# Turning the gated GLA output and half of the mixed activation by transposing DMAs of 16-bit words, in a two-layer encoder kernel

## The chip, the cores and the metric

The kernel runs on one core of a Trainium2 chip. The time is the device time of one execution in microseconds; of a kernel that ran several times the median is given. TensorE (PE) multiplies matrices, VectorE (DVE), ScalarE (ACT) and GpSimd (POOL) work on rows of up to 128 partitions, and SyncE (SP) issues the DMAs. Instructions of one engine run in the order in which they stand; engines wait for each other by semaphores.

## The reference

A trunk of two layers over 256 tokens of width 1024, all in float32. Per layer, cut to what matters here:

```
u = rms_norm(h) ; gq, gk, gv, gg, ra, aq, ak, av, gate_a, gate_b = split(u @ w_in)
o_gla   = rms_norm(gla(gq, gk, gv, ra)) * g_gla_out      # gated linear attention, both directions
branch_a = (o_gla * silu(gg)) @ w_o_gla
q, k    = rope(rms_norm(aq) * g_q_norm), rope(rms_norm(ak) * g_k_norm)
branch_b = attention(q, k, av) @ w_o_attn
mixed   = sigmoid(gate_a) * branch_a + sigmoid(gate_b) * branch_b
h = h + rms_norm(mixed @ w_out)
h = h + rms_norm(swiglu(rms_norm(h)))
h = h + rms_norm(sigmoid(h @ w_ple_gate) * (p[l] @ w_ple_proj))
```

## The kernel before

**Numbers in two parts.** A float32 value is held as a high part, rounded by a cast to a shorter TensorE format, and a low part, the rest. A product is three matmuls: high by high, high by low, low by high (`mm3`, whose matmuls are all recorded at L94). `split` makes the two parts: a cast on ScalarE (L110) and a subtract on VectorE (L106). This is done for the weights as they arrive and for every activation that goes into a product.

**Weights.** They come in units of 512 x 512 values (1 MB), on SP's queue, into two buffers named `raw`; `split` writes them into `wh` and `wl` (four buffers each). `Stream` keeps the order: a buffer that is released starts the next load, and the next split is cast when a `wh` is free. A unit serves 24 matmuls: four blocks of 128 rows, three products each, for two halves of 128 tokens.

**Stages.** Per layer: projections (rq, gqk, v), the attention branches running beside them as side work, then `gg` (the GLA's output gate), `gate` (the two branch gates), `merge` (both branch outputs and their mix), `wout`, `ffnin`, `ffnout`, `emb`, `ple`. The names in the profile carry the stage in which they were made: `wh_0gate` is a weight part of layer 0, cast in the gate stage. The gate stage has eight units, the merge stage eight.

**Turning activations.** An activation stands with tokens on partitions; as the left factor of the next product it needs its features on partitions. `transpose_in` turns 128 x 512 values: four TensorE transposes against an identity (L402) into a PSUM tile, then `put`, which splits the PSUM tile into the `Split` object's big tiles. A `Split` holds `makers`, the tasks that fill it, and `need` finishes them before the product that reads it. `gT` is the gated GLA output turned, `mixT` the mixed activation turned; for each there are two halves of tokens (`hf`) and two of features (`j`). `gT` is read by the first two units of the merge stage, `mixT` by `wout`.

**Order.** Side work is written as generators (`Task`): a `tick` after each six matmuls counts down, and a task goes on when its count is over; `yield 9` means nine ticks. A scheduler then sets each engine's order from the order of writing and priorities. `out_gate` computes the gated output per half `hf`: a sigmoid on ScalarE (L1156), two products on VectorE, then `turn_in`, a task of two `transpose_in`.

**Small tiles.** `t512()` gives a 128 x 512 tile from a ring of five. `rope_tables(l)` (L652) loads cosines, sines and two gains, and GpSimd multiplies them into two tables of 128 x 512 with buffers of their own. Layer 0's are made at the start, layer 1's after layer 0's merge stage. `inv_sqrt` and the tail of `row_rstd` (L452, L456) use GpSimd for the norms' roots: `rstd_0ffnout` is the scale of the norm behind layer 0's FFN.

Of the kernel before, what the change touches and what calls it, by code (L numbers as in the profile page):

```python
# [10 lines left out]
F32 = mybir.dt.float32  # L11
F32R = mybir.dt.float32r
BF16 = mybir.dt.bfloat16
AF = mybir.ActivationFunctionType
ALU = mybir.AluOpType
AX = mybir.AxisListType

P = 128
T = 256
D = 1024  # L20
DEPTH = 2
# [6 lines left out]
W = dict(r=5, z=6, s0=4, s=3, s1=9, o0=1, o=1, k=4, q=3, a0=1, a1=4, a2=4, a3=1, g=6)  # L28
# [10 lines left out]
OUT = (0, 1, 2, 3, 4, 5, 10, 6, 7, 8, 9)  # L39

WAIT_PAIR, WAIT_LAST = 9, (3, 4)
UNIT = 2112
RQ = ((0, 288), (288, 672), (672, 1056))
C_GQ, C_GK, C_GV, C_GG, C_RA = 0, 512, 1024, 2048, 3072
# [4 lines left out]
def trunk_kernel(ctx: ExitStack, tc: tile.TileContext, a: dict, out: bass.AP):  # L49
# [7 lines left out]
    nc = tc.nc  # L57
# [7 lines left out]
    smp = ctx.enter_context(tc.tile_pool(name="smp", bufs=4))  # L65
# [3 lines left out]
    part = ["start"]  # L69

    def nm(s):
        uid[0] += 1
        return f"{s}_{part[0]}_{uid[0]}"
# [10 lines left out]
    def aux():  # L84
        return accp.tile([P, 512], F32, tag="acc", name=nm("aux"))

    def t512():
        return smp.tile([P, 512], F32, tag="t512", name=nm("t512"), bufs=5)

    def small(n, tag, bufs=None):  # L90
        return smp.tile([P, n], F32, tag=tag, name=nm(tag), **({"bufs": bufs} if bufs else {}))
# [80 lines left out]
    for l in range(DEPTH):  # L172
        w = a["w_in"][l]
# [7 lines left out]
        w = a["w_ffn_in"][l]  # L181
# [179 lines left out]
    class Split:  # L361
# [26 lines left out]
        def put(self, src, k, n, t0, tn):  # L388

            split(*self.at(k, n, t0, tn), src.rearrange("p (k t) -> p k t", t=tn))  # L390

        def tok(self, k, hf):
            return [t[:, 0, :] for t in self.at(k, 1, hf * P, P)]

# [3 lines left out]
    def transpose_in(sp, src, k, n, hf, plain=None):  # L398

        ps = aux()  # L400
        for i in range(n):
            nc.tensor.transpose(ps[:, i * P : (i + 1) * P], src[:, i * P : (i + 1) * P], ident)  # L402
        with tc.high_priority(AHEAD):
            sp.put(ps[:, : n * P], k, n, hf * P, P)
        if plain is not None:
            nc.scalar.copy(plain, ps[:, : n * P])
# [15 lines left out]
    def row_rstd(parts, behind=None):  # L422
# [5 lines left out]
        for j, src in enumerate(parts):  # L428
# [9 lines left out]
            else:  # L438
                with tc.issue_after(behind.ins) if j and behind is not None else nullcontext():
                    last_square[0] = nc.scalar.activation(  # L440
                        junk[:, :n], src, AF.Square, scale=1.0 / 32.0, accum_out=ss[:, j : j + 1]
                    )
# [19 lines left out]
    def halves(t):  # L462
        return [t[:, j * 512 : (j + 1) * 512] for j in range(2)]

    def turn_in(sp, x, hf, wait, plain=None):


        def turn():
            yield wait
            for j, y in enumerate(halves(x)):  # L470
                transpose_in(sp, y, 4 * j, 4, hf, plain and plain[j])

        sp.makers[hf].append(Task(turn(), part[0]))
# [178 lines left out]
    def rope_tables(l):  # L652

        ropes = []
        tab = mid()
        cosT, sinT = (tab[:, i * 256 : (i + 1) * 256].rearrange("p (s d) -> p s d", d=P) for i in range(2))
        nc.sync.dma_start(cosT, a["rope_cos"].rearrange("(s p) d -> p s d", p=P))
        nc.sync.dma_start(sinT, a["rope_sin"].rearrange("(s p) d -> p s d", p=P))
        for i, gname in enumerate(("g_q_norm", "g_k_norm")):
            gn = gain(a[gname][l], tab[:, 512 + i * P : 512 + (i + 1) * P], P)  # L660
            rt = small(512, f"rope{i}", 1)
            ct, sn = (t.rearrange("p (s d) -> p s d", d=P) for t in (rt[:, 0:256], rt[:, 256:512]))
            nc.gpsimd.tensor_tensor(out=ct, in0=cosT, in1=gn.unsqueeze(1).broadcast_to([P, 2, P]), op=ALU.mult)
            quad = lambda t: t.rearrange("p (x y i) -> p x y i", x=2, y=2)
            for y in range(2):
                for hf in range(2):
                    nc.gpsimd.tensor_tensor(
                        out=quad(sn[:, hf, :])[:, :, y, :],
                        in0=quad(sinT[:, hf, :])[:, :, y, :],
                        in1=quad(gn)[:, :, 1 - y, :],  # L670
                        op=ALU.mult,
                    )
            ropes.append((ct, sn))
        return ropes

    def up_weights(l):

        up = mid()[0:81, :].rearrange("p (d c) -> p d c", d=2)
        wup = mid(F32R)[0:81, :].rearrange("p (d c) -> p d c", d=2)
        nc.gpsimd.memset(up, 0.0)  # L680
        for r in (0, 32, 64):
            nc.sync.dma_start(up[r : r + 16], a["w_alpha_up"][l].rearrange("d r c -> r d c"))
            nc.sync.dma_start(up[r + 16 : r + 17], a["b_alpha"][l].unsqueeze(0))
        nc.scalar.copy(wup, up)
        vsub(wup[64:81], up[64:81], wup[64:81].bitcast(F32))
        return wup
# [25 lines left out]
    def square(hf, j):  # L712
        on("act", nc.scalar.activation, t512(), hv(hf, j), AF.Square, scale=1.0 / 32.0, accum_out=ss[hf][:, j : j + 1])

# [58 lines left out]
    Task(start(), part[0])  # L773
    keep = cp.tile([P, 512], BF16, tag="keep", name="keep")
    nc.gpsimd.memset(keep, 1.0)
# [4 lines left out]
    for l in range(DEPTH):  # L780
# [3 lines left out]
        if l == 0:  # L784
            with after_start:
                ropes = rope_tables(0)
# [213 lines left out]
        for x in range(2):  # L1000
            o = project_t(uT)
            for i in range(2):
                dst = qk[:, x, 2 * i : 2 * i + 2, :]
                src = o[i].rearrange("p (h t) -> p h t", t=T)
# [143 lines left out]
        gT = Split()  # L1148

        def out_gate():  # L1150
            while not (gla.over and attention.over):
                yield 1
            for hf in range(2):
                sg = mid()
                with tc.issue_after(last_exp[0].ins):
                    nc.scalar.activation(sg, gg[:, hf, :], AF.Sigmoid)  # L1156
                for j, t in enumerate(halves(sg)):
                    s = slice(j * 512, (j + 1) * 512)
                    vmul(t, t, gg[:, hf, s])
                    vmul(t, t, on[:, hf, s])  # L1160
                turn_in(gT, sg, hf, W["g"])

        ogate = Task(out_gate(), f"{l}gg")

# [3 lines left out]
        for br in range(2):  # L1168
            t = big().rearrange("p (s c) -> p s c", s=2)
# [8 lines left out]
        mixT = Split()  # L1178
        ogate.need()
        for j in range(2):  # L1180
            for br, src in enumerate((gT, aT)):
                for hf, o in enumerate(project(src)):
                    sl = [s[:, hf, j * 512 : (j + 1) * 512] for s in sgate]
                    vmul(sl[br], o, sl[br])
                    if br == 1:
                        nc.vector.tensor_tensor(out=sl[0], in0=sl[0], in1=sl[1], op=ALU.add)

                        def turn(src=sl[0], j=j, hf=hf):
                            yield WAIT_MIX
                            transpose_in(mixT, src, 4 * j, 4, hf)  # L1190

                        mixT.makers[hf].append(Task(turn(), part[0], j))

        if l + 1 < DEPTH:
            ropes = rope_tables(l + 1)


        part[0] = f"{l}wout"
        gpost = gain(a["g_mix_post"][l], mid(), D)
# [24 lines left out]
        for hf in range(2):  # L1224
            ws.lend = hf == 1
            for b in range(2):
# [5 lines left out]
                sg = t512()  # L1232
# [75 lines left out]
        for x in FFN:  # L1308
# [7 lines left out]
            if x == "o":  # L1316
                n, w = outs.pop(0), ws.take()
# [8 lines left out]

        if l + 1 < DEPTH:
            wup_next = up_weights(l + 1)


        part[0] = f"{l}ffnout"
# [17 lines left out]
        for hf in range(2):  # L1349
            s = slice(hf * P, (hf + 1) * P)  # L1350
# [85 lines left out]
```

## Time and profile before

| what | value |
|---|---|
| median of 3 runs | 939.79 us (938.04 to 939.82) |
| the profiled execution | span 937.3 us; the page gives no further time of it |
| TensorE busy | 922.6 us, 98% of the span, 4697 instructions |
| VectorE, ScalarE, GpSimd busy | 732.4, 561.6 and 80.8 us |
| DMA, all of it | 169.26 MB, 181 GB/s over the span |
| TensorE clock granted | 0.9 or more in every slice of the span |

The profile is of one execution. Its span runs from the first to the last recorded instruction; the median is 2.5 us above it. A matmul's row has the engine, the line, the output and the two inputs, the weights' and the moving operand's shapes. Transposes on TensorE stand as matmuls with `ident`. "The chain" is the work that ended last, followed back from the end.

### The profile page before, as it was taken

Reading aid. Unit: us, or ns where it says so; the run is one execution under the profiler, and the core shown is the slowest. Engines: PE = TensorE matmul, PEld = TensorE weight load, DVE = VectorE, ACT = ScalarE, POOL = GpSimd, SP = SyncE. Lnnn points to the kernel's source line nnn. Section 1 sums busy time; section 2 is a strip of 40 time slices with the busy share of each in tenths; the row PEclk is TensorE's granted clock in tenths of the full one; section 3 lists DMA queues with packets and bytes.
Section 4 is the critical chain, followed back from the end, with each engine's and each line's share of the span. In section 5 each row is a group of like instructions: output and inputs, shape, how many; then the busy total and the mean of one; then the engine's idle time right before and its main releaser. Section 6 shows DMA issues by size and latency. Waiting matters only on the chain.

```text
span 937.3 us, 12331 instructions
## 1 busy us (share of the span) xinstructions
PE 922.6 (98%) x4697; PEld 783.9 (84%) x4697; DVE 732.4 (78%) x933; ACT 561.6 (60%) x928; POOL 80.8 (9%) x150
## 2 busy tenths in 40 slices
PE   8999999999999999999999999999999999999996
PEld 6998888888878878888899988888888788888786
DVE  4798978456569899999689799674666798989874
ACT  4669676443457565567666686754435666656563
POOL 3400214000000000000022001200001000000000
PEclk9999999999999999999999999999999999999999
DMA  6464455665275565547455525365553937463551
GB/s 229 168 223 137 136 191 191 191 213 180 91 249 169 203 233 190 203 143 249 167 175 181 192 78 180 116 244 181 200 190 103 310 114 268 154 266 112 180 180 45
DMA packets 88089, 169.26 MB, mean 181 GB/s; under 512 B 3351, under 2 KB 26391, under 8 KB 88030
## 3 DMA queue, kind: packets, MB, share of 16 engines
q1 hardware_dynamic: 88030, 168.47, 52.8%
q8 instruction: 37, 0.61, 0.3%
q14 instruction: 22, 0.18, 0.1%
HBM read 167.41 MB, written 1.05 MB: 180 GB/s over the span
## 4 chain that ended last, share of the span: by engine, by line
PE 79%; DVE 9%; DMA 4%; ACT 3%; issue 3%; POOL 1%; SPq 0%; POOLq 0%; ACTq 0%; DVEq 0%
PE acc_1ffnin L94 9%; PE acc_0ffnin L94 8%; PE acc_0gate L94 5%; PE acc_1gate L94 5%; PE acc_1merge L94 5%; PE acc_0merge L94 5%; PE acc_0ffnin L543 4%; PE acc_1ffnin L543 4%; PE acc_1gqk L94 2%; PE acc_0rq L94 2%; PE acc_0gqk L94 2%; PE acc_1ple L94 2%; PE acc_0gg L94 2%; PE acc_1gg L94 2%; PE acc_1v L94 2%
## 5 line engine op out<-in xcount | busy, mean ns | idle before, releaser
L94 PE MATMUL acc_1ffnin<-wh_1ffnin,big_1ffnin 128*128 128x512 f32 x176 | 56.9, 393 | 0.0
L94 PE MATMUL acc_0ffnin<-wh_0ffnin,big_0ffnin 128*128 128x512 f32 x176 | 56.8, 392 | 0.0
L110 ACT CAST wh_1ffnin<-raw_1ffnin 128x1024 fp32r<-128x1024 f32 x38 | 38.1, 1050 | 23.1 <-PE acc_1ffnin L94 7.7
L110 ACT CAST wh_0ffnin<-raw_0ffnin 128x1024 fp32r<-128x1024 f32 x38 | 37.9, 1049 | 22.0 <-PE acc_0ffnin L94 7.9
L106 DVE TENSOR_TENSOR wl_1ffnin<-raw_1ffnin,wh_1ffnin 128x1024 fp32r<-128x1024 f32 x38 | 44.8, 1219 | 5.6 <-ACT wh_1ffnin L110 5.4
L106 DVE TENSOR_TENSOR wl_0ffnin<-raw_0ffnin,wh_0ffnin 128x1024 fp32r<-128x1024 f32 x38 | 44.7, 1219 | 3.9 <-ACT wh_0ffnin L110 3.9
L94 PEld LDWEIGHTS acc_1ffnin<-wh_1ffnin,big_1ffnin 128*128 128x128 f32 x176 | 33.0, 188 | 7.1 <-ACT big_1ffnin L110 0.4
L94 PEld LDWEIGHTS acc_0ffnin<-wh_0ffnin,big_0ffnin 128*128 128x128 f32 x176 | 33.0, 188 | 6.7
L106 DVE TENSOR_TENSOR wl_0ffnin<-lent_0ffnin,wh_0ffnin 128x1024 fp32r<-128x1024 f32 x30 | 35.5, 1218 | 1.9 <-ACT wh_0ffnin L110 1.7
L106 DVE TENSOR_TENSOR wl_1ffnin<-lent_1ffnin,wh_1ffnin 128x1024 fp32r<-128x1024 f32 x30 | 35.4, 1218 | 2.0 <-ACT wh_1ffnin L110 2.0
L110 ACT CAST wh_1ffnin<-lent_1ffnin 128x1024 fp32r<-128x1024 f32 x30 | 30.2, 1049 | 9.0 <-PE acc_1ffnin L94 3.0
L110 ACT CAST wh_0ffnin<-lent_0ffnin 128x1024 fp32r<-128x1024 f32 x30 | 30.2, 1049 | 8.4 <-PE acc_0ffnin L94 3.7
L94 PE MATMUL acc_0ffnin<-wl_0ffnin,big_0ffnin 128*128 128x512 f32 x88 | 34.3, 389 | 0.0
L94 PE MATMUL acc_1ffnin<-wl_1ffnin,big_1ffnin 128*128 128x512 f32 x88 | 34.3, 389 | 0.0
L94 PE MATMUL acc_1ffnin<-wh_1ffnin,big_1wout 128*128 128x512 f32 x96 | 31.2, 394 | 0.0
L94 PE MATMUL acc_0ffnin<-wh_0ffnin,big_0wout 128*128 128x512 f32 x96 | 31.2, 394 | 0.0
L543 PE MATMUL acc_0ffnin<-wh_0ffnin,mid_0ffnin 128*128 128x512 f32 x96 | 31.0, 390 | 0.0
L543 PE MATMUL acc_1ffnin<-wh_1ffnin,mid_1ffnin 128*128 128x512 f32 x96 | 31.0, 390 | 0.0
L106 DVE TENSOR_TENSOR wl_0gate<-raw_0gate,wh_0gate 128x1024 fp32r<-128x1024 f32 x14 | 16.5, 1221 | 17.8 <-ACT wh_0gate L110 17.8
L106 DVE TENSOR_TENSOR wl_1gate<-raw_1gate,wh_1gate 128x1024 fp32r<-128x1024 f32 x14 | 16.5, 1221 | 17.8 <-ACT wh_1gate L110 17.8
L94 PE MATMUL acc_0rq<-wh_start,big_start 128*128 128x384 f32 (+1 forms) x96 | 25.4, 349 | 1.4 <-ACT big_start L120 1.4
L94 PE MATMUL acc_0gate<-wh_0gate,big_start 128*128 128x512 f32 x80 | 24.8, 389 | 0.0
(647 smaller groups left out, 2931.3 us busy)
## 6 DMA issues: line engine op xcount, KB each, us to landing
raw_0ffnin<-in_w_ffn_out_dram SPq DMA_DIRECT2D x11, 1024.0 KB, 5.3
raw_1ffnin<-in_w_ffn_out_dram SPq DMA_DIRECT2D x11, 1024.0 KB, 5.9
lent_0ffnin<-in_w_ffn_in_dram SPq DMA_DIRECT2D x6, 1024.0 KB, 8.7
lent_1ffnin<-in_w_ffn_in_dram SPq DMA_DIRECT2D x6, 1024.0 KB, 7.8
raw_0rq<-in_w_in_dram SPq DMA_DIRECT2D x4, 1024.0 KB, 5.2
raw_0v<-in_w_in_dram SPq DMA_DIRECT2D x4, 1024.0 KB, 5.0
raw_0gg<-in_w_in_dram SPq DMA_DIRECT2D x4, 1024.0 KB, 5.1
raw_0gate<-in_w_o_gla_dram SPq DMA_DIRECT2D x4, 1024.0 KB, 5.2
```

The source lines that it names most:

```text
L94: return nc.tensor.matmul(o, lhsT, rhs, start=start, stop=stop)
L106: nc.vector.tensor_tensor(out=out, in0=in0, in1=in1, op=ALU.subtract)
L110: nc.scalar.copy(hi, src)
L543: nc.tensor.matmul(o, x, y, start=first and k + n == 0, stop=k == 3 and n == 2, skip_group_check=not first)
```

## The change

Three edits.

- `turn_words` takes the place of TensorE's transposes for all four pieces of `gT` and for the first feature half of `mixT` (two pieces): six pieces per layer, twelve in all. A piece of 128 x 512 float32 is seen as 128 x 1024 words of 16 bits. A ScalarE copy sets the low words first and the high words behind them (`w`), a transposing DMA on SP's queue turns the eight blocks of 128 x 128 words (`r`), and a ScalarE copy interleaves the words again (`z`), which `put` splits. Between these steps it waits 3 and 9 ticks (`SENT`, `LANDED`), and between two pieces of the gated output 2 (`NEXT`). The second feature half of `mixT` stays on TensorE.
- The ring of `t512` has seven tiles instead of five; the rope tables are taken from it instead of from buffers of their own.
- Layer 1's `rope_tables` are made at the end of `ffnin`, not at the end of `merge`.

```
 WAIT_PAIR, WAIT_LAST = 9, (3, 4)
+SENT, LANDED, NEXT = 3, 9, 2
...
-        return smp.tile([P, 512], F32, tag="t512", name=nm("t512"), bufs=5)
+        return smp.tile([P, 512], F32, tag="t512", name=nm("t512"), bufs=7)
...
+        def turn_words(self, src, k, n, hf):
+            x = lambda: t512()[:, : n * P]
+            w = x()
+            w16 = w.bitcast(U16)
+            nc.scalar.copy(
+                w16.rearrange("p (s c) -> p s c", s=2), src.bitcast(U16).rearrange("p (c s) -> p s c", s=2)
+            )
+            yield SENT
+            r = x()
+            r16 = r.bitcast(U16)
+            nc.sync.dma_start_transpose(out=r16.rearrange("p (r t) -> p r t", t=P), in_=w16)
+            yield LANDED
+            z = x()
+            z16 = z.bitcast(U16)
+            nc.scalar.copy(z16.rearrange("p (c s) -> p s c", s=2), r16.rearrange("p (s c) -> p s c", s=2))
+            self.put(z, k, n, hf * P, P)
...
-            rt = small(512, f"rope{i}", 1)
+            rt = t512()
...
-                turn_in(gT, sg, hf, W["g"])
+                for j, y in enumerate(halves(sg)):
+                    gT.makers[hf].append(Task(gT.turn_words(y, 4 * j, 4, hf), part[0], j))
+                    yield NEXT
...
-                        def turn(src=sl[0], j=j, hf=hf):
+                        def turn(src=sl[0], hf=hf):
                             yield WAIT_MIX
-                            transpose_in(mixT, src, 4 * j, 4, hf)
-
-                        mixT.makers[hf].append(Task(turn(), part[0], j))
-
-        if l + 1 < DEPTH:
-            ropes = rope_tables(l + 1)
-
+                            transpose_in(mixT, src, 4, 4, hf)
+
+                        turn = turn() if j else mixT.turn_words(sl[0], 0, 4, hf)
+                        mixT.makers[hf].append(Task(turn, part[0], j))
...
             wup_next = up_weights(l + 1)
+            ropes = rope_tables(l + 1)
```

How this moves instructions is seen at two places. SP's queue, from the load of the gate stage's fourth unit (`raw_0gg_1470`) to that of its eighth (`raw_0gate_1726`), before:

```order
L257 DMA raw_0gg_1470<-in_w_in_dram 128x4x512
L657 DMA mid_0merge_2228<-in_rope_cos_dram 128x2x128
L658 DMA mid_0merge_2228<-in_rope_sin_dram 128x2x128
L257 DMA raw_0gg_1598<-in_w_in_dram 128x4x512
L328 DMA mid_0merge_2228<-in_g_q_norm_dram 128x128
L328 DMA mid_0merge_2228<-in_g_k_norm_dram 128x128
L328 DMA mid_0wout_2245<-in_g_mix_post_dram 128x1024
L328 DMA mid_0wout_2247<-in_g_ffn_pre_dram 128x1024
L257 DMA raw_0gate_1656<-in_w_in_dram 128x4x512
L257 DMA raw_0gate_1664<-in_w_in_dram 128x4x512
L328 DMA ggla_1gla_4863<-in_g_gla_out_dram 128x256
L257 DMA raw_0gate_1726<-in_w_in_dram 128x4x512
```

The rope loads and gains stand between the weights; all are plain loads. The same stretch in the changed kernel, up to the first unit of the merge stage (names are numbered anew; `t_` is a `t512` tile, and lines are two further down):

```order
L259 DMA raw_0gg_1470<-in_w_in_dram 128x4x512
L410 DMA_TRANSPOSE t_0gg_1670<-t_0gg_1632 128x8x128
L259 DMA raw_0gg_1598<-in_w_in_dram 128x4x512
L330 DMA mid_0wout_2234<-in_g_mix_post_dram 128x1024
L259 DMA raw_0gate_1654<-in_w_in_dram 128x4x512
L410 DMA_TRANSPOSE t_0gg_1692<-t_0gg_1646 128x8x128
L259 DMA raw_0gate_1662<-in_w_in_dram 128x4x512
L410 DMA_TRANSPOSE t_0gg_1720<-t_0gg_1684 128x8x128
L410 DMA_TRANSPOSE t_0gg_1734<-t_0gg_1700 128x8x128
L259 DMA raw_0gate_1708<-in_w_in_dram 128x4x512
L330 DMA mid_0wout_2236<-in_g_ffn_pre_dram 128x1024
L259 DMA raw_0gate_1748<-in_w_o_gla_dram 128x4x512
```

The rope loads are gone from here, and four transposing DMAs stand between the weights: one ahead of unit five, one between units six and seven, two ahead of unit eight (`raw_0gate_1708`).

GpSimd's queue at the end of layer 0's FFN, before:

```order
L680 MEMSET mid_0ffnin_3709 81x1024
L452 TENSOR_SCALAR rstd_0ffnout_3775<-ss_0ffnout_3774 128x1
L456 TENSOR_TENSOR rstd_0ffnout_3775<-rstd_0ffnout_3775,neghalf 128x1
L452 TENSOR_SCALAR rstd_0ffnout_3863<-ss_0ffnout_3862 128x1
L456 TENSOR_TENSOR rstd_0ffnout_3863<-rstd_0ffnout_3863,neghalf 128x1
```

And in the changed kernel (`t_0ffnin` are the rope tables, `mid_0ffnin_3709` what was loaded for them):

```order
L688 TENSOR_TENSOR t_0ffnin_3713<-mid_0ffnin_3709 128x256
L692 TENSOR_TENSOR t_0ffnin_3713<-mid_0ffnin_3709 128x2x32 x4
L688 TENSOR_TENSOR t_0ffnin_3720<-mid_0ffnin_3709 128x256
L692 TENSOR_TENSOR t_0ffnin_3720<-mid_0ffnin_3709 128x2x32 x4
L477 TENSOR_SCALAR rstd_0ffnout_3781<-ss_0ffnout_3780 128x1
L481 TENSOR_TENSOR rstd_0ffnout_3781<-rstd_0ffnout_3781,neghalf 128x1
```

The tables' ten operations now stand ahead of the norm's.

More of the change, by code (lines that the diff above doesn't have):

```diff
@@ L13 @@
 BF16 = mybir.dt.bfloat16
+U16 = mybir.dt.uint16
 AF = mybir.ActivationFunctionType
```

## The prediction

> **What bounds the kernel now.** First the page's line of busy times and the chain's shares by engine; then the stretches in which the transposes lie (the gate and merge stages of both layers), by engine; then the chain inside them.
>
> ```profile
> PE 922.6 (98%) x4697; PEld 783.9 (84%) x4697; DVE 732.4 (78%) x933; ACT 561.6 (60%) x928; POOL 80.8 (9%) x150
> PE 79%; DVE 9%; DMA 4%; ACT 3%; issue 3%; POOL 1%; SPq 0%; POOLq 0%; ACTq 0%; DVEq 0%
> ...
> 144.00:192.00 48.00, 48.00 (x226) 39.97 (x226) 29.68 (x34) 26.40 (x37) 10.38 (x15) 1.00 0.62 204
> 192.00:236.50 44.50, 44.50 (x203) 36.91 (x201) 26.63 (x28) 17.61 (x19) 0.00 (x0) 1.00 0.57 191
> 603.00:651.00 48.00, 48.00 (x225) 39.94 (x224) 29.68 (x34) 26.16 (x36) 2.77 (x5) 1.00 0.55 189
> 651.00:695.40 44.40, 44.40 (x202) 36.86 (x201) 26.63 (x28) 17.61 (x19) 0.00 (x0) 1.00 0.57 191
> ...
> 157.83 1.75 PE aux_0gg L402 x16
> 218.09 0.87 PE aux_0merge L402 x8
> 616.60 1.75 PE aux_1gg L402 x16
> 676.86 0.87 PE aux_1merge L402 x8
> ```
>
> The window rows give stretch, length, then busy time of PE, PEld, DVE, ACT and POOL, granted clock, DMA share and GB/s. TensorE is busy in the whole of all four windows at a granted clock of 1.00; VectorE has some 18 us to spare in each, ScalarE 22 to 27. So here every TensorE instruction lengthens the kernel, and a weight that comes late would do so too. The chain names the groups removed: 16 and 8 transposes per layer (layer 0's 16 last 1.75 us, 109 ns each).
>
> **Removed: 48 transposes.** 2 × (1.75 + 0.87) = 5.24 us, all on the path. Their own rows, with the pipeline's fill, read 1.91 and 1.03 us; two layers at those would be 5.88. I take the chain's 5.24.
>
> ```profile
> 157.67 1.91 PE L402 MATMUL aux_0gg<-ident,mid_0gg 128*128 128x128 f32 x16
> 159.33 0.47 PE L94 MATMUL acc_0gate<-wh_0gg,big_start 128*128 128x512 f32 x1
> 192.08 0.39 PE L94 MATMUL acc_0merge<-wh_0gate,big_0gg 128*128 128x512 f32 x1
> 217.93 1.03 PE L402 MATMUL aux_0merge<-ident,big_0gate 128*128 128x128 f32 x8
> ```
>
> **Added: two ScalarE copies a turn.** Twelve per layer, of 1024 16-bit elements a partition. None is in the trace; the nearest row is ScalarE on 1024 elements, SBUF to SBUF.
>
> ```profile
> 147.12 1.06 ACT L1156 ACTIVATE mid_0gg<-big_0gg 128x1024 f32<-128x1024 f32 x1
> 153.72 2.00 ACT L110 CAST wh_0gate<-raw_0gg 128x1024 fp32r<-128x1024 f32 x2 [3.18 <-DMA raw_0gg<-in_w_in_dram]
> 170.52 2.01 ACT L110 CAST wh_0gate<-raw_0gate 128x1024 fp32r<-128x1024 f32 x2 [2.12 <-PE acc_0gate L94]
> 154.72 3.49 DVE L106 TENSOR_TENSOR wl_0gate<-raw_0gg,wh_0gate 128x1024 fp32r<-128x1024 f32 x3
> 214.04 2.00 ACT L110 CAST wh_0merge<-raw_0merge 128x1024 fp32r<-128x1024 f32 x2 [3.43 <-PE acc_0merge L94]
> ```
>
> At 1.06 us each ScalarE goes from 26.4 to 34.9 of the gate's 48 us and from 17.6 to 21.8 of the merge's 44.5. What it delays are weight casts, and these run ahead: between 159.33 and 192.08 lie six units of 24 matmuls, 5.44 us each; the cast at 170.52 is the eighth gate unit's and waits for TensorE to release a buffer; its unit is used at 192.08 − 5.44 = 186.6. That lead of some 14 us is the cover; without it each copy would cost its 1.06. The cast and subtract behind each turn stay, reading SBUF instead of PSUM: nothing.
>
> **Added: the transposing DMA's place in SP's queue.** A turn has time: gT, whose transposes ran at 157.67, is read at 192.08; the mixed activation's first half, turned at 217.93, some 18 us later. The question is what it holds up: weights wait behind it on the same queue.
>
> ```profile
> 142.57 0.68 DVE L103 TENSOR_TENSOR mid_0gg<-mid_0gg,big_0gla 128x512 f32<-128x512 f32 x1
> 148.62 0.37 SPq L257 DMA_DIRECT2D raw_0gg<-in_w_in_dram  x1
> 155.96 2.65 SPq L257 DMA_DIRECT2D raw_0gate<-in_w_in_dram  x2
> 164.42 0.37 SPq L257 DMA_DIRECT2D raw_0gate<-in_w_in_dram  x1
> ...
> raw_0gate<-in_w_in_dram SPq DMA_DIRECT2D x2, 1024.0 KB, 4.9
> ...
> DMA packets 361, 0.17 MB, mean 169 GB/s; under 512 B 31, under 2 KB 361, under 8 KB 361
> q1 hardware_dynamic: 361, 0.17, 57.4%
> DMA packets 200, 0.41 MB, mean 410 GB/s; under 512 B 0, under 2 KB 0, under 8 KB 200
> q1 hardware_dynamic: 200, 0.41, 105.8%
> ```
>
> A packet window's rows give packets, MB and share of the 16 engines' time: the first window is one microsecond of small loads (140 to 141), the second one of weights (138 to 139).
>
> The first transposing DMA stands ahead of the load at 148.62; its words follow the product that ends at 143.25, so it is issued near 145. The second stands between the two loads of 155.96 (units six and seven), the third and fourth ahead of unit eight's, at 164.42.
>
> How long one of 256 KB holds the queue (call it t) no row shows. Below: at 410 GB/s, 0.64 us. Above: if it goes in pieces of 32 bytes, 8192 of them; the first window, of 1 us, gives 0.574 × 16 / 361 = 25.4 ns a packet of about 512 bytes, and over 16 engines at that 13.0 us. Between: 1024 rows of 256 bytes at 25.4 ns are 1.63 us, my value, since that is the size of a block's row here.
>
> Unit six lands at 155.96 + 4.9 = 160.9. Behind it come t, unit seven (1 MB at 410 GB/s, 2.6 us), 2t, unit eight (2.6) and its split (3.3: two casts and the last subtract): ready at 169.4 + 3t. It is needed at 186.6 − 1.75 = 184.9. So t up to 5.2 us costs nothing; above, 3(t − 5.2) per layer. In the merge two transposes stand between a load and the second output unit's; words ready near 214.5 and 217.5, that load's landing near 217: ready 217 + 2t + 5.9 (2.6 and 3.3 again), needed near 238.3 (192.08 + eight units of 5.44 + 0.87 is 236.5, where the output begins; its second unit follows half a unit, 2.7, later; all 0.87 sooner now). Up to 7.7 us nothing, then 2(t − 7.7). At 1.63 both are free, by 10.6 and 12 us.
>
> The row of 109 ns a block on TensorE comes first; the Trainium skill ("VectorE: DVE Perf Modes", The three transpose paths) lists a DMA transpose of a 128×128 block of 16-bit words at 1309 ns and advises TensorE wherever the result may go to PSUM. Eight blocks in turn would be an estimate of 10.5 us, and by it the sum would be 2 × (15.9 + 5.6) − 4.9 = 38 us slower, about 978. No run so far shows that price. The Trainium skill ("DMA: Bandwidth & Descriptors", Latency and other measured facts) also gives 261 GB/s to a transposing DMA, an estimate of 1.0 us, which leaves the sum as it is.
>
> **Moved: the next layer's rope tables, now at the end of the FFN's first part.** Their loads stand behind the embedding projection's and ahead of a gain; their ten POOL operations stand ahead of the one that gives the FFN's post-norm.
>
> ```profile
> 154.35 4.43 POOL L663 TENSOR_TENSOR rope_0merge<-mid_0merge 128x256 f32<-128x256 f32 x1 [5.21 <-DMA mid_0merge<-in_g_q_norm_dram]
> 158.75 1.16 POOL L667 TENSOR_TENSOR rope_0merge<-mid_0merge 128x64 f32<-128x64 f32 x4
> 159.87 0.74 POOL L663 TENSOR_TENSOR rope_0merge<-mid_0merge 128x256 f32<-128x256 f32 x1
> 160.56 1.18 POOL L667 TENSOR_TENSOR rope_0merge<-mid_0merge 128x64 f32<-128x64 f32 x4
> ...
> 425.64 0.37 SPq L257 DMA_DIRECT2D raw_0ffnin<-in_w_ple_proj_dram  x1
> 426.10 0.42 SPq L328 DMA_DIRECT2D mid_0ffnout<-in_g_ple_post_dram  x1
> mid_0ffnout<-in_g_ple_post_dram SPq DMA_DIRECT2D x1, 512.0 KB, 5.8
> ...
> 434.35 0.30 POOL L452 TENSOR_SCALAR rstd_0ffnout<-ss_0ffnout 128x1 f32<-128x1 f32 x1 [48.19 <-ACT t_0ffnout L440]
> 434.74 0.57 POOL L456 TENSOR_TENSOR rstd_0ffnout<-rstd_0ffnout,neghalf 128x1 f32<-128x1 f32 x1
> 435.51 1.41 DVE L500 SCALAR_TENSOR_TENSOR h<-mid_0ffnout,rstd_0ffnout,h 128x512 f32<-128x512 f32 x2
> 439.82 1.03 PE L402 MATMUL aux_0ffnout<-ident,h 128*128 128x128 f32 x8
> 447.52 0.39 PE L94 MATMUL acc_0ple<-wh_0ffnout,big_0ffnout 128*128 128x512 f32 x1
> ```
>
> The tables' inputs land about where that gain did, 426.1 + 5.8 = 431.9, or half a microsecond earlier. Beside three VectorE subtracts the chain took 7.4 us (154.35 to 161.74); with all operations as fast as the later ones it is 2 × (0.74 + 1.17) = 3.8. VectorE is busy there too: I take a middle end, 437.5 to 438.2. Then 0.95 for the norm (0.30 + 0.57 and a gap) and 0.7 a half of h: first half at 439.2 to 439.9, against 439.82. A stall of 0 to 0.3; taken 0.3. With the slow chain (end 439.3) it is about 1.2, with inputs 1.8 us late 3. Behind h on VectorE wait two units' splits (four subtracts of 1.17 us, as in the row of three) and those of the turned h (two of half that size, 0.6 each): 5.9 us from about 440.6 to 446.5, in time for the embedding's first product at 447.52, by 1 us. On SP the tables' loads delay the gain at 426.10 by their own small size alone, and the tables aren't read before the next layer. There is one such place, since only layer 0 makes tables for a next layer. The old place in the merge ran beside busy TensorE: nothing comes back.
>
> Seven 512-column tiles instead of five, plus the two tables' own: more turns in flight at no time of an engine.
>
> **Sum.** 937.3 (the span) − 5.24 + 0.3 = 932.4. The median shown, 939.79, is 2.5 above that span; so 934.9 us.
>
> **The rivals.**
> 1. The transposing DMA goes in small pieces, holds the queue, and weights come late. For it: pieces as small as 32 bytes give 13 us. Against: the row-sized pieces give 1.63, and the lead of units is long. Gain and loss balance at t = 5.2 + 4.94/6 = 6.0 us; above it the kernel is slower, 939.8 at 6.0 and 939.79 − 4.94 + 2 × (23.4 + 10.6) = 1002.9 at 13. Chance 0.14.
> 2. The eight blocks of one transposition are turned one after the other, each with a latency of its own. The load of 1 MB shows a fixed part of 4.9 − 2.6 = 2.3 us; were each block to pay half of it, t would be 9.2 us and the time 934.9 + 2 × (3 × 4.0 + 2 × 1.5) = 965. Against: it is one instruction on the queue, and loads of many rows pay that part once. Chance 0.08. The Trainium skill's 1309 ns a block (as above) is of this size, and its advice would be right here.
> 3. The tables on POOL hold up h: the gain is less by 1 to 3 us, 935.8 to 937.6. For it: the 4.43 us operation beside VectorE's subtracts. Chance 0.10.
> 4. TensorE's freed time isn't given back, as VectorE or ScalarE sets the pace, or t lies between 5.7 and 6.3: within 0.2%, 939.8. Against: both have 18 us or more idle in each window. Chance 0.08.
>
> **How the numbers follow.** My forecast has 0.60. About 0.2%, 1.88 us, is what a measurement of this kernel can tell from no change: 937.91 to 941.67. Rival 3 and the forecast lie below it: faster 0.70, same 0.08 (rival 4), slower 0.22 (rivals 1 and 2). The forecast's own range is 933.5 (5.88 saved with no stall gives 933.9) to 936. The whole range, for 8 in 10, leaves out 0.16 of rivals 1 and 2 above 944 (t over 6.7 us) and a little below 932.8.
>
> **What would show it.** No L402 rows under the gated output; TensorE at 100% of both stages, which end 1.75 and 0.87 us sooner per layer; casts there still released by TensorE, not by a DMA; two copies of about 1.06 us a turn; transposes landing within 5 us of issue. Wrong if casts of the gate stage wait on loads, TensorE shows gaps before a unit, or the transpose of h starts over 1 us late against the matmuls around it.

## The result, and the profile after

| | median | runs |
|---|---|---|
| changed kernel | 931.49 us | 930.93 to 933.16, 4 runs |
| kernel before, beside it | 938.91 us | 937.94 to 939.82, 4 runs |
| ratio | 0.993 | 95% interval 0.9914 to 0.9946 |

Faster by 7.4 us, where 4.9 were forecast; the time lies 1.3 us below the stated range. The two kernels were compared twice more, later: 933.51 against 938.21 us (ratio 0.9947, 0.9932 to 0.9963) and 934.49 against 938.13 us (0.9959, 0.9942 to 0.9976). So the gain is 3.6 to 7.4 us by the medians; all 16 runs of the changed kernel have a median of 933.73 us, the 61 of the kernel before in the later comparisons one of 937.90. Three of the first four runs of the changed kernel lie below all twelve later ones (932.55 and more); what set them apart isn't shown.

The page of the changed kernel, its line of busy times and the chain's shares by engine:

```profile
PE 916.4 (99%) x4649; PEld 777.9 (84%) x4649; DVE 732.8 (79%) x933; ACT 587.4 (63%) x952; POOL 82.3 (9%) x150
...
PE 81%; DVE 9%; DMA 3%; ACT 2%; issue 2%; POOL 1%; SPq 0%; POOLq 0%; ACTq 0%; DVEq 0%
```

TensorE has 48 instructions less (4697 to 4649) and 6.2 us less to do; ScalarE 24 more and 25.8 us more; VectorE stands as it was. The span is 929.6 us, the profiled execution's time 931.35, 1.75 more.

The gate and merge stages of the changed kernel, as windows from the first matmul of each stage to that of the next (columns as in the prediction's windows):

```profile
143.20:188.95 45.75, 45.75 (x207) 37.80 (x206) 29.57 (x34) 33.94 (x45) 2.74 (x4) 1.00 0.80 234
188.95:232.45 43.50, 43.50 (x193) 36.03 (x192) 26.57 (x28) 22.03 (x23) 0.00 (x0) 1.00 0.65 207
599.10:644.85 45.75, 45.75 (x206) 37.81 (x205) 29.67 (x34) 34.05 (x45) 2.73 (x4) 1.00 0.80 231
644.85:688.35 43.50, 43.50 (x193) 36.05 (x192) 26.62 (x28) 22.18 (x23) 0.00 (x0) 1.00 0.65 207
```

TensorE is still busy in the whole of every window at a clock of 1.00: nothing that was added reached it. ScalarE's 33.9 and 22.0 us are near the 34.9 and 21.8 forecast.

The limits of these windows, from the timelines of the kernel before (the first two rows) and of the changed kernel:

```profile
144.51 0.39 PE L94 MATMUL acc_0gate<-wh_0gg,big_start 128*128 128x512 f32 x1
...
236.50 0.39 PE L94 MATMUL acc_0wout<-wh_0merge,big_0merge 128*128 128x512 f32 x1
```

```profile
143.19 0.39 PE L96 MATMUL acc_0gate<-wh_0gg,big_start 128*128 128x512 f32 x1
...
188.94 0.39 PE L96 MATMUL acc_0merge<-wh_0gate,big_0gg 128*128 128x512 f32 x1
...
232.46 0.39 PE L96 MATMUL acc_0wout<-wh_0merge,big_0merge 128*128 128x512 f32 x1
```

With the row at 192.08 of the prediction, the gate stage went from 47.57 to 45.75 us and the merge from 44.42 to 43.52. The same differences between first matmuls, for seven profiles (us; "start" is the time of layer 0's first keys-and-values matmul):

| profile | start | gate 0 | merge 0 | ffnin 0 | gate 1 | merge 1 | ffnin 1 |
|---|---|---|---|---|---|---|---|
| before | 38.76 | 47.57 | 44.42 | 181.70 | 47.57 | 44.41 | 182.38 |
| before_again (same kernel) | 36.98 | 47.57 | 44.41 | 181.69 | 47.57 | 44.41 | 181.28 |
| ropes_only | 37.38 | 47.57 | 44.41 | 183.02 | 47.57 | 44.41 | 181.54 |
| gated_only | 37.99 | 45.74 | 44.43 | 182.22 | 45.74 | 44.43 | 181.49 |
| after | 37.35 | 45.75 | 43.52 | 181.37 | 45.76 | 43.52 | 181.41 |
| after_again (same kernel) | 37.82 | 45.75 | 43.52 | 182.95 | 45.75 | 43.52 | 182.48 |
| after_third (same kernel) | 37.50 | 45.76 | 43.52 | 183.96 | 45.74 | 43.52 | 181.98 |

In these profiles the gate stage is 1.82 us shorter wherever the gated output is turned by DMA, the merge 0.90 wherever the mix is, to 0.02 us: 2 × (1.82 + 0.90) = 5.44 us. What else differs is in the start and in the two FFNs, and there the same kernel differs from itself by up to 2.6 us. The whole time shows less of the gain than the stages do: 937.90 − 933.73 is 4.2 us. Where the other 1.3 us go, or whether they are scatter, is open.

The transposing DMA. Its queue's row on the page of before and then on that of after (packets, MB, share of 16 engines' span):

```profile
q1 hardware_dynamic: 88030, 168.47, 52.8%
```

```profile
q1 hardware_dynamic: 100702, 171.62, 55.8%
```

And the turn's own instructions in the changed kernel (line, count, duration in ns as least, median and greatest), with the DMAs' median time from issue to landing behind the name in the last two rows:

```profile
L410 SPq DMA_TRANSPOSE t_0gg<-t_0gg x4: 1237/1294/5613, 143.1 to 158.9; - x4
...
L410 SPq DMA_TRANSPOSE t_0merge<-t_0merge x2: 1232/1242/1252, 211.3 to 214.2; - x2
```

```profile
L404 ACT COPY t_0gg<-mid_0gg x4: 1034/1042/1058, 142.0 to 156.2; 128x1024 uint16<-128x1024 uint16 x4
```

```profile
L414 ACT COPY t_0gg<-t_0gg x4: 1348/1358/1364, 159.8 to 170.1; 128x1024 uint16<-128x1024 uint16 x4
```

```profile
t_0gg<-t_0gg SPq DMA_TRANSPOSE x4, 7.7
...
t_0merge<-t_0merge SPq DMA_TRANSPOSE x2, 3.1
```

12,672 packets more are 1056 a piece; 0.558 × 929.6 − 0.528 × 937.3 = 23.8 us of the queue's time, an estimate of 1.98 us a piece, where 1.63 was taken. A piece lands 3.1 us after its issue in the merge and 7.7 in the busier gate stage, where the prediction had looked for 5. The Trainium skill ("VectorE: DVE Perf Modes", The three transpose paths) prices a block at 1309 ns; the trace doesn't agree for eight blocks in one instruction, of which all together took 2.0 us of the queue and, in the merge, 3.1 us from issue to landing. 256 KB in 1.98 us are 132 GB/s; the trace gives half of the 261 of the Trainium skill ("DMA: Bandwidth & Descriptors", Latency and other measured facts), the lower of the two rates there.

The cover in the gate stage, from the changed kernel's timelines of SP and VectorE:

```profile
157.51 6.97 SPq L410 DMA_TRANSPOSE t_0gg<-t_0gg  x2
164.59 0.52 SPq L259 DMA_DIRECT2D raw_0gate<-in_w_in_dram  x1
```

```profile
172.37 2.36 DVE L108 TENSOR_TENSOR wl_0gate<-raw_0gate,wh_0gate 128x1024 fp32r<-128x1024 f32 x2 [2.69 <-ACT wh_0gate L112]
```

Unit eight's load goes out at 164.59, behind two transposes whose issue took SP 7 us; its split is done at 174.7 and it is used at 188.94 − 5.44 = 183.5. The lead is 8.8 us; 10.6 were forecast.

On the way, unit seven's cast waited for its load, where before it had waited for TensorE. From ScalarE's timelines, before and after:

```profile
165.08 2.01 ACT L110 CAST wh_0gate<-raw_0gate 128x1024 fp32r<-128x1024 f32 x2 [1.64 <-PE acc_0gate L94]
```

```profile
164.74 2.00 ACT L112 CAST wh_0gate<-raw_0gate 128x1024 fp32r<-128x1024 f32 x2 [2.89 <-DMA raw_0gate<-in_w_in_dram]
```

The prediction had named casts that wait on loads as a sign that it is wrong. The sign came, and TensorE didn't wait: a late cast costs only what goes beyond the lead.

The moved tables, from the changed kernel's timelines of GpSimd, VectorE and TensorE:

```profile
428.49 0.85 POOL L688 TENSOR_TENSOR t_0ffnin<-mid_0ffnin 128x256 f32<-128x256 f32 x1 [46.82 <-DMA mid_0ffnin<-in_g_q_norm_dram]
...
433.36 0.30 POOL L477 TENSOR_SCALAR rstd_0ffnout<-ss_0ffnout 128x1 f32<-128x1 f32 x1
433.75 0.57 POOL L481 TENSOR_TENSOR rstd_0ffnout<-rstd_0ffnout,neghalf 128x1 f32<-128x1 f32 x1
```

```profile
434.35 1.41 DVE L525 SCALAR_TENSOR_TENSOR h<-mid_0ffnout,rstd_0ffnout,h 128x512 f32<-128x512 f32 x2 [2.73 <-POOL rstd_0ffnout L481]
```

```profile
435.33 1.15 PE L427 MATMUL aux_0ffnout<-ident,h 128*128 128x128 f32 x8
```

The tables took 4.8 us (3.8 to 7.4 were the bounds), h came 2.7 us later than VectorE would have had it, and its first half was ready at 435.05, 0.28 us ahead of TensorE. The eight transposes took 1.15 us instead of 1.03: a stall of 0.1.

### The profile page after: what moved, and what is told of

It is laid out like the page before. It is cut to its first block, busy times and chain, and to the rows that moved or that the text cites. A ratio compares the mean times of both kernels' runs of the same rounds, so it can differ in the third digit from the quotient of the medians.

```text
span 929.6 us, 12279 instructions
## 1 busy us (share of the span) xinstructions
PE 916.4 (99%) x4649; PEld 777.9 (84%) x4649; DVE 732.8 (79%) x933; ACT 587.4 (63%) x952; POOL 82.3 (9%) x150
## 4 chain that ended last, share of the span: by engine, by line
PE 81%; DVE 9%; DMA 3%; ACT 2%; issue 2%; POOL 1%; SPq 0%; POOLq 0%; ACTq 0%; DVEq 0%
PE acc_0ffnin L96 11%; PE acc_1ffnin L96 7%; PE acc_0ffnin L568 6%; PE acc_0gate L96 5%; PE acc_1gate L96 5%; PE acc_1merge L96 5%; PE acc_0merge L96 5%; DVE wl_1ffnin L108 4%; PE acc_1ffnin L568 3%; PE acc_1gqk L96 2%; PE acc_0gqk L96 2%; PE acc_1ple L96 2%; PE acc_0rq L96 2%; PE acc_0gg L96 2%; PE acc_1gg L96 2%; PE acc_0v L96 2%
## 5 line engine op out<-in xcount | busy, mean ns | idle before, releaser
L96 PE MATMUL acc_1gate<-wh_1gate,big_0ple 128*128 128x512 f32 x80 | 24.8, 389 | 0.0
```

Source lines behind the costliest of these rows:

```text
L96: return nc.tensor.matmul(o, lhsT, rhs, start=start, stop=stop)
```

## The experiments

The question after the result: do the 2 us beyond TensorE's own 5.4 belong to the change? Theory A: no, they are scatter between executions of any of these kernels. Theory B: yes, from the ring of seven or the moved tables.

**before_again.** No edit: the kernel before.

> The kernel before, unchanged, for a second profile. Theory A (the 2 us beyond the transposes' own time are scatter between executions: the start and the last FFN's waits for weights): its start (the first six transposes near 16.1 us in the first profile, 14.9 in the changed kernel's) or its wait of 1.48 us on VectorE near 884.9 differ here from the first profile by about 1 us; the span may lie anywhere from 935.5 to 938. Theory B (those 2 us come with the ring of seven tiles or the moved tables): both stand as in the first profile within 0.3 us, span 937 to 938.

936.14 us, a single run, span 934.4, 1.1 us below what theory A allowed and 2.6 below B's. Two rows of the first profile of before, and then the same instructions in this one, from TensorE's timelines:

```profile
16.14 0.95 PE L120 MATMUL aux_start<-ident,mid_start 128*128 128x128 f32 x6
...
884.88 0.66 PE L402 MATMUL aux_1ffnin<-ident,t_1ffnin 128*128 128x128 f32 x4 [1.48 <-DVE t_1ffnin L103]
```

```profile
14.51 0.82 PE L120 MATMUL aux_start<-ident,mid_start 128*128 128x128 f32 x6
...
882.02 0.66 PE L402 MATMUL aux_1ffnin<-ident,t_1ffnin 128*128 128x128 f32 x4
```

The start is 1.6 us earlier and the wait of 1.48 us is gone, with nothing changed. In the changed kernel's profile these were the two places that had gained (14.88, no wait). So what they gave there needs no cause in the change: A, not B, for these two. What makes them differ between executions isn't shown.

**ropes_only.** The kernel before, with

```
-        ... tag="t512", name=nm("t512"), bufs=5)
+        ... tag="t512", name=nm("t512"), bufs=7)
-            rt = small(512, f"rope{i}", 1)
+            rt = t512()
         (and rope_tables(l + 1) moved from the end of merge to the end of ffnin)
```

> The kernel before with the ring of seven 512-column tiles and the rope tables taken from it and made at the end of ffnin; all transposes stay on TensorE. Theory A: as before within 1 us, 938 to 939.5. Theory B: 2 to 2.5 us faster than before, 936.5. If the tables on GpSimd hold up h (rival 3 of the prediction): 0.3 to 3 us slower, 939.2 to 942.

937.61 us against 938.21, ratio 0.9994 (0.9981 to 1.0008): no difference. B's 2 us faster are excluded by a little (the interval ends at 1.8 us faster), rival 3's slowing of 0.3 us isn't (it ends at 0.75 us slower).

**ropes_back.** The changed kernel, with

```
+        if l + 1 < DEPTH:
+            ropes = rope_tables(l + 1)          # at the end of merge again
...
-            ropes = rope_tables(l + 1)          # at the end of ffnin
```

> The changed kernel with layer 1's tables made after the merge again (still in the ring of seven). Theory A: as the changed kernel within 0.7 us, 931.5. Theory B, if the tables' place made the 2 us: 933.5. If the tables held up h in the changed kernel: 931.2 or less.

933.09 us, ratio 0.9942 (0.9928 to 0.9955), within the changed kernel's own runs. By the numbers written down beforehand this is B's 933.5; but they started from the first measurement's 931.5, and the same kernel without the edit later took 933.51 and 934.49 (below). So this run doesn't separate A from B, and shows only that the tables' place is worth nothing that these runs can tell.

**gated_only.** The changed kernel, with

```
-                        turn = turn() if j else mixT.turn_words(sl[0], 0, 4, hf)
-                        mixT.makers[hf].append(Task(turn, part[0], j))
+                        mixT.makers[hf].append(Task(turn(), part[0], j))    # turns both j on TensorE
```

> The changed kernel with the mixed activation's first half turned on TensorE again; the gated output stays with the DMAs. TensorE gets 16 transposes back, 0.9 us per layer: 931.5 + 1.8 = 933.3 under A and B alike. If the two transposing DMAs in the merge had cost anything by holding up weights, less than that: 932.5.

934.27 us, ratio 0.9954 (0.9941 to 0.9966). That is 1.0 us above the number expected, which also started from 931.5. Beside the changed kernel's median over all runs it is 0.5 us slower, which scatter hides; the table shows the 0.9 us in both merges (44.43), the gate stages shortened as before, and no more.

**after_again** and **after_third.** No edit: the changed kernel.

> The changed kernel, unchanged, beside the kernel before on the same chip, for the size of the gain. If the gain is the transposes' own time (5.4 us on TensorE): 938.2 - 5.4 = 932.8. If the first measurement's 7.4 us belongs to the change: 930.8.

> The changed kernel once more, for the size of the gain with more runs: 5.0 to 5.4 us under the kernel before beside it if the transposes' time is all of it, so 932.3 to 933.2; 930.5 to 931.5 if the first measurement's 7.4 us holds.

933.51 and 934.49 us. The first measurement's 931.49 was the low end. The gains beside the kernel before are 4.70 and 3.64 us: neither is the first measurement's 7.4, and after_third stays 1.4 us short of the 5.0 that were expected at least. After_third differs from the first profile most in layer 0's FFN (183.96 against 181.37 us); there its TensorE waits, and behind that ScalarE waits for weights. From its timeline, its waits of ScalarE between 255 and 345 us (us in total, times, longest), and the same waits in before_again:

```profile
329.45 0.47 PE L568 MATMUL acc_0ffnin<-wh_0ffnin,big_0wout 128*128 128x512 f32 x1 [1.11 <-DVE mid_0ffnin L607]
```

```profile
ACT wh_0ffnin L112 <- DMA raw_0ffnin<-in_w_ffn_in_dram: 3.7, 2, 1.9
```

```profile
ACT wh_0ffnin L110 <- DMA raw_0ffnin<-in_w_ffn_in_dram: 0.7, 1, 0.7
```

Weights of the FFN land at the edge of being needed, and these two executions wait there 3.7 and 0.7 us. It isn't the only place: in ropes_only the FFN took 183.0 us with 0.8 us of such waits. Whether the changed kernel waits there more on the average stays open: three profiles of it give 181.4, 183.0 and 184.0 us, two of the kernel before 181.7 both. Twice the turning work doesn't lengthen it: the changed kernel with copies doubled gives 181.6, with transposing DMAs doubled 181.4 (both below).

**ropes_twice.** The changed kernel, with each GpSimd operation of layer 1's tables done twice:

```
-            nc.gpsimd.tensor_tensor(out=ct, ...)
+            for _ in range(1 + (l > 0)):
+                nc.gpsimd.tensor_tensor(out=ct, ...)
-            for y in range(2):
+            for y in (0, 1) * (1 + (l > 0)):
```

> The changed kernel in which GpSimd makes layer 1's tables twice over (ten more operations, 4 to 5 us by the changed kernel's rows), ahead of the norm's root. If h ends only 0.3 us ahead of TensorE's transposes of it, as the changed kernel's rows say: 3.5 to 4.5 us slower than the changed kernel, 936. If VectorE's or the loads' later waits have room for it: within 1 us of the changed kernel.

938.96 us, 5.5 slower than after_again, 1 more than the first branch allowed. TensorE's row, and two windows, the first from within the wait:

```profile
439.53 1.50 PE L427 MATMUL aux_0ffnout<-ident,h 128*128 128x128 f32 x8 [3.28 <-DVE h L525]
```

```profile
438.00:442.00 4.00, 2.46 (x11) 2.03 (x12) 3.27 (x4) 1.52 (x3) 0.61 (x2) 0.82 0.00 0
442.00:446.00 4.00, 4.00 (x15) 3.12 (x15) 4.00 (x6) 3.30 (x7) 0.86 (x2) 0.76 0.56 179
```

The wait is there, 3.28 us. Most of the other 2.2 us is the granted clock of 0.82 and 0.76: over the 2.46 and 4.00 us that TensorE was busy in these windows, an estimate of 2.46 × 0.18 + 4.00 × 0.24 = 1.4 us. So h was at the edge in the changed kernel, as its rows said: rival 3's mechanism is there, and the changed kernel was 0.28 us short of it.

**times2** and **times3.** The changed kernel, with

```
-            nc.sync.dma_start_transpose(out=r16..., in_=w16)
+            for _ in range(2):        # times3: 3
+                nc.sync.dma_start_transpose(out=r16..., in_=w16)
```

> The changed kernel with every transposing DMA issued twice with the same words into the same tile; the second of a pair waits on SP until the first has landed. By the changed kernel's packets one holds the queue 2.0 us. If only time on the queue counts, free up to 5.2 us a turn in the gate stage: 4.0 us cost nothing, as the changed kernel, 931.5 to 932.8. If SP's waits for landings (about 5 us each, four in a gate stage) count against a lead of some 15 us: 0 to 5 us per layer, up to 942, with casts of the gate stage waiting on weight loads.

> The same with three issues of each. By queue time alone 6.0 us a turn, over the free 5.2 by 0.8: 3 x 0.8 x 2 = 4.9 us slower than the changed kernel, 937. If SP's waits count: eight landings of 5 us in a gate stage, 25 us more than the lead, per layer: 950 to 985.

times2: 932.13 us, no cost. But the repeated issues don't all stand where the sum has them. SP's timeline of times2, from unit six's load to what follows unit eight's:

```profile
152.64 0.37 SPq L259 DMA_DIRECT2D raw_0gate<-in_w_in_dram  x1
153.07 6.99 SPq L411 DMA_TRANSPOSE t_0gg<-t_0gg  x2
160.15 0.53 SPq L259 DMA_DIRECT2D raw_0gate<-in_w_in_dram  x1
161.14 1.23 SPq L411 DMA_TRANSPOSE t_0gg<-t_0gg  x1
163.65 0.38 SPq L259 DMA_DIRECT2D raw_0gate<-in_w_in_dram  x1
164.07 5.92 SPq L411 DMA_TRANSPOSE t_0gg<-t_0gg  x2
```

Three transposes stand between unit six's load and unit eight's, as many as in the changed kernel. Of the four that were added in this stage one stands ahead of unit six's load and three behind unit eight's; in times3, too, only three stand between the two loads. So neither run tests the limit of 5.2 us a turn. What times2 shows is that eight transposes in a gate stage and four in a merge cost nothing. By the pages' queue rows (58.5% of 931.1 us, 59.3% of 948.3) the second pieces took 2.2 us each of the queue and the third ones 1.5, so the 1.98 is known to about half a microsecond.

times3: 947.61 us, 14 slower, but not where it was expected: its gate stages are 45.75 us, as in the changed kernel. The merge grows by 2.7 and 4.1 us and wout by 4.1 and 5.7. From its TensorE and ScalarE timelines, and a window behind the wait:

```profile
235.44 0.50 PE L96 MATMUL acc_0wout<-wh_0merge,big_0merge 128*128 128x512 f32 x1 [2.58 <-ACT big_0merge L112]
...
243.97 0.66 PE L428 MATMUL aux_0merge<-ident,big_0gate 128*128 128x128 f32 x4 [1.84 <-DVE big_0gate L1214]
```

```profile
232.40 2.51 ACT L415 COPY t_0merge<-t_0merge 128x1024 uint16<-128x1024 uint16 x2 [4.41 <-DMA t_0merge<-t_0merge]
```

```profile
235.40:239.40 4.00, 3.96 (x10) 2.86 (x11) 3.81 (x5) 4.00 (x5) 0.00 (x0) 0.62 0.19 71
```

What comes late is the turned mix itself, not a weight: ScalarE's interleaving copies wait 4.41 us for the transposes, whose six issues stand among weight loads, and `wout` waits for the cast behind them. After 2.6 us of waiting the clock is 0.62 for 4 us; that (1.5 us, an estimate of 3.96 × 0.38) and the second wait of 1.84 are most of what `wout` grows by in layer 0. Both expectations failed on the place: queue time (937) and SP's waits ahead of weights (950 to 985).

**stores8.** The changed kernel, with eight stores of the turn's source behind each transposing DMA, into the output, which is written at the end:

```
             nc.sync.dma_start_transpose(out=r16..., in_=w16)
+            for i in range(8):
+                s = slice(i // 2 % 2 * 512, (i // 2 % 2 + 1) * 512)
+                nc.sync.dma_start(out[0, i % 2 * P : (i % 2 + 1) * P, s], src)
```

> The changed kernel in which each of the twelve turns also stores its source eight times (256 KB each) into the output, which the kernel overwrites at its end: 2 MB more per turn on SP's queue, 5.2 us at 410 GB/s. By the order, 24 of a gate stage's stores and three transposes stand between units seven's load and that of the merge's first unit. By the prediction's queue sum with 2.0 us a transpose: that unit is ready at 160.9 + 0.7 + 2.0 + 2.6 + 5.2 + 2.6 + 2 x (2.0 + 5.2) + 2.6 + 3.3 = 194.3 against 190.3 needed, in the time of the profile before: TensorE waits 4 us a layer ahead of the merge, 932.7 + 8 = 941, with casts waiting on loads of w_o_gla. If the gate stage has more lead than that sum says: within 2 us of the changed kernel. If stores are slower than loads: above 945.

965.27 us, ratio 1.0294 (1.0266 to 1.0322). From its timelines of TensorE and ScalarE, and a window of it:

```profile
195.04 1.22 PE L96 MATMUL acc_0merge<-wh_0gate,big_0gg 128*128 128x512 f32 x2 [5.50 <-ACT wh_0gate L112]
```

```profile
193.94 1.99 ACT L112 CAST wh_0gate<-raw_0gate 128x1024 fp32r<-128x1024 f32 x2 [5.74 <-DMA raw_0gate<-in_w_o_gla_dram]
```

```profile
190.00:200.00 10.00, 4.92 (x13) 3.46 (x14) 4.68 (x4) 4.47 (x5) 0.00 (x0) 0.66 0.92 323
```

This is rival 1 made real, at the place that was named: the cast of the merge's first weights waits for their load, and TensorE for the cast, 5.5 us where 4 were worked out. The queue was made long by stores, not by transposes, so this shows what a late weight does, not how long a transposing DMA holds the queue. The time fell into the third branch, above 945: the sum took 410 GB/s, and between 150 and 190 us the queue moved 271 to 331 with the DMA engines busy for 0.93 or more of each 10 us. What the sum lacked besides is what follows: slow clock, and the merge (47.7 us against 43.5) and wout (27.6 against 23.9) late in turn.

**copies_twice.** The changed kernel, each ScalarE copy of a turn in a loop of two:

```
+            for _ in range(2):
                 nc.scalar.copy(w16..., src...)
...
+            for _ in range(2):
                 nc.scalar.copy(z16..., r16...)
```

> The changed kernel with both ScalarE copies of each turn done twice (24 more copies, 29 us of ScalarE's time at 1.04 and 1.35 us). If the copies lie beside TensorE's work as the prediction says: as the changed kernel, 931.5 to 933.5. If weight casts behind them were near the edge: 1 to 10 us slower, with TensorE waiting on casts in the gate stage.

933.15 us, ratio 0.9949 (0.9929 to 0.9968): as the changed kernel. ScalarE had room for twice as much; the prediction's zero for the copies holds.

**queries_too.** A try at a faster version: the second head group's queries turned by DMA as well.

```
+        def send_q(hf):                     # w, yield SENT, transposing DMA into early[hf]
...
             for hf in range(2):
                 yield W["q"]
+                if g:                       # z from early[hf], split into qh, ql
...
-                (four TensorE transposes of the second group, each hf)
```

> The changed kernel in which the second head group's queries (two pieces of 128 x 512 per layer, 16 transposes in all) are turned by transposing DMAs too, sent while the first group's attention runs. If a turn with slack gains just TensorE's time: 16 x 0.109 = 1.75 us faster than the changed kernel's pooled 932.5, 930.8. If its two tiles or copies hold up the attention, which runs beside the projections: 932.5 or slower, with TensorE waiting in the GLA or the gate stage.

935.93 us, ratio 0.9983 (0.9969 to 0.9996): slower than the changed kernel by 2.2 us. TensorE's waits in it:

```profile
91.35 0.74 PE L96 MATMUL aux_0at<-mid_0at,big_0kv 128*128 128x512 f32 x2 [0.57 <-DVE mid_0at L108]
...
98.85 0.50 PE L96 MATMUL acc_0v<-wh_0gqk,big_start 128*128 128x512 f32 x1 [0.62 <-DVE big_0at L108]
...
547.47 0.73 PE L96 MATMUL aux_1at<-mid_1at,big_1kv 128*128 128x512 f32 x2 [0.85 <-DVE mid_1at L108]
...
554.97 0.50 PE L96 MATMUL acc_1v<-wh_1gqk,big_0ple 128*128 128x512 f32 x1 [0.66 <-DVE big_1at L108]
```

None of these is in the changed kernel: 1.2 and 1.5 us a layer of waits for the attention's VectorE work. Nor did TensorE's own work get shorter: from the first gqk matmul to the first of the merge it is busy for 0.04 and 0.13 us a layer less than in the changed kernel, not for 0.87, with 16 instructions less in all (4633). The stages gqk and v lose instructions, while gg is 0.86 and 0.81 us longer and gate 0.96 and 0.98 (46.71 and 46.74), with side work that came in later. Why the removed transposes saved no time here is open. None of these kernels is faster than the changed one by more than the scatter.

## Why the prediction was right or wrong

- **The transposes' 5.24 us on the path: right.** 5.44 by the stages, in all seven profiles, between the chain's 5.24 and the rows' 5.88; gated_only separates the merge's part.
- **Added on ScalarE at no cost: right**, and copies_twice shows room for as much again. The interleaving copy was mis-sized: 1.36 us, not 1.06.
- **The transposing DMA's place in the queue at no cost: right.** 1.98 us a piece, not 1.63, which the lead covers. Two of the signs named for it failed without harm: a cast of the gate stage waited 2.89 us on a load, and pieces there landed after 7.7 us, not within 5. The limit of 5.2 us a turn wasn't tested; stores8 shows only that the mechanism of rival 1 exists. It was worked out for weights alone, and in times3 the first to be late was the turned mix.
- **The tables' stall of 0.3 us: right in kind**, 0.1 in the profile; ropes_twice shows that there was no more than 0.3 us of room. Neither ropes_only nor ropes_back moved the time by anything that these runs can tell.
- **From span to median: wrong.** This step failed: "The median shown, 939.79, is 2.5 above that span; so 934.9 us", and with it the range. It takes the one span of 937.3 us as fixed except for the change, and 2.5 us as what lies between a span and a time. The runs show 1.66 to 1.99 us between the two, 1.75 in the changed kernel's profiled execution; by that the rest of the 2.5 is the difference between the profiled execution and the median one. And of the 7.7 us between the spans of 937.3 and 929.6 the gate and merge stages are 5.4, the start 1.4 and the two FFNs 1.3 (0.4 go the other way elsewhere): before_again has the faster start, and no wait of 1.48 us, with nothing changed. The range was made from unknown costs alone, and three runs from 938.04 to 939.82 were taken as the kernel's time. In the four later comparisons the kernel before ran from 935.24 to 941.16 us, with medians of 938.21, 938.21, 937.66 and 938.13. A scatter of this size belonged into the range on both sides: 938 − 4.94 is 933.1, and the changed kernel's 16 runs go from 930.93 to 935.08. The gain forecast, 4.94, lies among the three measured, 7.42, 4.70 and 3.64; that the first was 2 us over the stages' 5.44 was luck.
- **Rivals 2 and 4** were not met: a piece took 2.0 us of the queue, not 9.2, and TensorE's freed time is there at the end of both stages.

## What to carry to other kernels

Where one engine is busy through a whole stage, instructions taken off it can be worth their own time, as in the gate and merge stages here (2.72 us a layer, 2.62 forecast), if the substitute's engine and queue have a lead that is worked out place by place; queries_too shows that it isn't so everywhere. Look for the lead of the result itself, not only of what stands behind it in the queue. When an experiment repeats an instruction, look in its trace where the repeats stand. Three runs aren't a kernel's time: compare stage by stage between two profiles of the same kernel before putting a gain of 2 us in 940 down to a change. And a wait on the busiest engine can cost more than its length, since the granted clock may fall behind it.

## What the runs showed of the hardware

- After TensorE had waited 2.6 us (times3) the granted clock was 0.62 over the next 4 us; in the 4 us in which a wait of 3.3 ended (ropes_twice) it was 0.82 and in the next 4 us 0.76; in the 10 us around a wait of 5.5 (stores8) 0.66. Behind shorter waits both occur: 1.00 over 2 us after 1.48 (before, at 884.9) and over 4 us after 1.84 (times3, at 244.0), but 0.67 and then 0.50 over 2 us each after 1.83 (stores8, at 242.7).
- Issuing a transposing DMA took SP at least 1.23 us in the changed kernel, and 7 us for two in the busy gate stage, where loads of 1 MB were issued in 0.37 to 0.52; the load behind those two went out when they were done (164.59).
- ScalarE's copy of 1024 16-bit words cost 1.04 us when it separates the words and 1.36 when it interleaves them, though both read and write the same amount.
